# Two attentions that share a memory map: the masks move to the constants, the sums of values to other pools

## The chip, the cores and the metric

The kernel runs on one core of one Trainium2 chip. The metric is the device time of one execution in microseconds. The core has a matrix engine (PE, with its weight loads listed apart as PEld), a vector engine (DVE), a scalar engine (ACT), GpSimd (POOL), and a queue SP from which all transfers of this kernel are issued. Each engine and the queue run their instructions in the order of the program; one that waits holds up all that stand behind it on the same engine. Operands stand in the on-chip memory, which has 128 partitions; addresses below are bytes in a partition.

## The reference

One layer of a hybrid encoder on a sequence of 1024 tokens of width 1024, in float32:

```python
h = rmsnorm(x, attn_norm_g)
(c_q, c_kv, k_rope, z_mla, q_dil, k_dil, v_dil, z_dil, g_mla, g_dil) = jnp.split(h @ w_in, split_points, axis=-1)
a_out = mla_attention(c_q, c_kv, k_rope, positions, mla_q_norm_g, mla_kv_norm_g, w_uq, w_ukv)
y_mla = (a_out * jax.nn.silu(z_mla)) @ w_o_mla
d_out = dilated_mixture(q_dil, k_dil, v_dil, positions)
y_dil = (d_out * jax.nn.silu(z_dil)) @ w_o_dil
merged = gate_mla * y_mla + gate_dil * y_dil
return x + merged @ w_out
```

A final rmsnorm follows. The latent attention has 8 heads, dense and bidirectional; the dilated mixture has 3 groups of 8 heads, of dilation 1, 4 and 16. In the dilated groups every query sees keys within a window only; the kernel adds a mask to the scores for the groups of dilation 1 and 4. The three groups' outputs are combined with softmax weights made of their denominators.

## The kernel before

Every float32 product is made of three matmuls of rounded parts (`mm3`, lines 71 to 73): each operand is split into a high part `_h` (a cast on ACT, line 77) and a low part `_l` (a subtraction, line 78, on DVE or POOL). Every transfer goes through `dma` (line 67), on SP.

The stages, in order of time:

1. `latent_proj`, `tables` and `token_factors` (from 0 us): x is loaded and scaled into `hT_h`, `hT_l`, the latent projections are made, the rotary tables and the row factors R. Then `latents` and `dil_v`, which store q, k and v in DRAM.
2. `blocks`: the projections of q and k of the dilated heads, 12 items (3 groups, two halves of the heads, q and k). The last item is k of the group of dilation 16. `block_steps` copies its result on ACT (line 509) to two tiles `dq_st00` and `dq_st10` and stores them by eight transfers to `s_dk`, the first four from `dq_st00`, the last four from `dq_st10`. Between the engines this stage has an order written out by hand.
3. `dil_attention`: four pairs of heads, for each pair the groups 0, 1, 2. For groups 0 and 1, `dil_head` loads q, k, v (`op_b`, `op_a`, `op_c`), makes scores on PE (lines 808 and 809) into PSUM tiles `s_ps`, and `soft_block` (line 777) adds the mask on DVE, writes `p`, and writes the row minimum into a column of a small tile `d_st`; ACT makes the exponential (line 778). The two halves of an `s_ps` share a bank, so the scores of the second half are written only when line 777 has read the first. `p` is transposed on PE (line 816), split (for group 0 into two large tiles `pt0_h`, `pt0_l`, whose borders POOL sets to zero once, line 1114) and multiplied with v; `av_sum` (line 771) puts the sum into `num`. `combine` weighs and adds the three `num` of a pair (DVE line 964, POOL line 966) and stores the first to `s_da`.
4. `mla_attention`: eight heads in four pairs; `av_sum` writes into a `num` of the pair, `mla_finish` multiplies it with the denominators and stores it to `s_ma` (for the last pair it goes into `brm_h`, `brm_l`, lines 760, 77 and 78).
5. `output`: the last projections and the normalisation. Its gates (`gate`), the rows of w_out (`wo_raw`) and its operands take the memory of the closed pools.

A generator, `fillers`, gives PE other work meanwhile: projections of z and of the gates (tiles `w_raw`, `w_h`, `w_l` for the weights, `pj` in PSUM, `zg_z` and `zg_t` for the result; lines 598 to 605), then the output projection of the dilated branch. 19 steps of it (FIRST_FEED) stand ahead of the dilated attention, the others are handed out behind score and transpose matmuls. From the end of the dilated attention each filler also runs a `piece` (line 582): it loads a part of `s_da` and of z into a `zg_z` and a `zg_t`, multiplies them, and splits the product into `brd_h` (ACT) and `brd_l` (POOL).

The program is written with tiles from pools; outside `blocks` a planner decides the order of each engine's instructions from a simulated run of the program, with the program's order as priority. A tile's place in memory follows from the pools: pools of the left side stand above each other in the order in which they are opened, those of the right side below each other from the top, and inside a pool the tiles stand in the order of their first use, each with its number of buffers. Pools are closed and others opened in their place (`reuse_waits="tile"`): the first write to a tile then waits until the old tiles that lay on the same bytes are done with, and on no others. The places that matter, as the program has them:

| pool (side) | tile: bytes |
|---|---|
| const (left) | warm, consts, rcol: to 1856 |
| op (left, stages 3 and 4) | 1856 to 43840 |
| ap (left, stages 3 and 4) | num 43840 to 60224 (4 x 4096); p, av_t, pt_h, pt_l, bc, m_nm, m_den, m_d to 93312 |
| dx (left, stage 3) | masks 93312; pt0_h 98432; pt0_l 108160; d_st 117888 (2 x 384); c_sn 118656; c_w 121728; c_d 123776 to 125312 |
| brd (left, stage 4) | brd_h 93312; brd_l 109696 to 126080 |
| dt (right, stage 2) | w_raw 75744; st_c 83936; st_t 88032; rope_m0 90080; rope_m1 92128; dq_st00 94176; dq_st10 98272; dq_st01 102368; dq_st11 106464 to 110560 |
| cosd (right, stages 1 and 2) | cs_d 110560 to 118752 |
| zt (right, fillers) | zg_z 126944, 128992; zg_t 131040, 133088 |
| brm (right, from the second part of the fillers) | brm_h 131040, brm_l 147424 to 163808 |
| output (left) | wout_h 10048, wout_l 42816, mg_l 75584, gate 108352 (5 x 2048), wo_raw 118592 (3 x 2048) to 124736 |

Stage 3 has its `num` in four buffers, of which a pair uses three; lines 1108 and 1109 make the tile of the masks, 128 x 1280 float32, as the first of dx and issue its transfer.

Of the kernel before, what the change touches and what calls it, by code (L numbers as in the profile page):

```python
# [10 lines left out]
F32 = mybir.dt.float32  # L11
F32R = mybir.dt.float32r
# [4 lines left out]
PSUM = bass.MemoryType.PSUM  # L17
DRAM = bass.MemoryType.DRAM

S = 1024  # L20
# [31 lines left out]
class Net:  # L52
# [616 lines left out]
    def mla_attention(self, ap, pp):  # L669
        nc = self.nc  # L670
        v = nc.vector
        for pair in range(4):
            num = ap.tile([128, S], F32, name="num", bufs=4)
            nm = ap.tile([128, 2, 8], F32, name="m_nm", bufs=2)
            den = ap.tile([128, 2, 8], F32, name="m_den", bufs=2)
            for hh in range(2):
# [10 lines left out]
                for u in range(4):  # L687
# [3 lines left out]
                    for b2 in range(2):  # L691
# [9 lines left out]
                        p = ap.tile([128, S], F32, name="p", bufs=3)  # L701
# [196 lines left out]
    def dil_attention(self, ap, dx, pp):  # L898
        nc = self.nc
        v = nc.vector  # L900
        for pair in range(4):
            st = dx.tile([128, 3, 2, 2, 8], F32, name="d_st", bufs=2)
            nums = []
            for g in range(3):
                num = ap.tile([128, S], F32, name="num", bufs=4)
                if g == 2:
                    self.dil_classes(pair, st, num, ap, pp)
                    nums.append(num)
                    continue
                for hh in range(2):  # L910
                    self.dil_head(g, pair * 2 + hh, hh, st, num, ap, pp)
                nums.append(num)
            self.combine(pair, st, nums, ap, dx, pp)
# [125 lines left out]
    def run(self):  # L1039
        tc, nc = self.tc, self.nc  # L1040
        with ExitStack() as ctx:
# [12 lines left out]
            cp = ctx.enter_context(tc.tile_pool(name="const", reuse_waits="tile", bufs=1))  # L1054
# [11 lines left out]
            with tc.tile_pool(name="wpx", reuse_waits="tile", bufs=2, side="right") as self.wpx, tc.tile_pool(name="cosd", reuse_waits="tile", bufs=1, side="right") as dpool, ExitStack() as sums:  # L1066
                with tc.tile_pool(name="pj_a", reuse_waits="tile", bufs=NB_A, space=PSUM) as pj, tc.tile_pool(name="dvp", reuse_waits="tile", bufs=3, side="right") as vp:
                    with tc.tile_pool(name="lp", reuse_waits="tile", bufs=1) as lp, tc.tile_pool(name="pj_l", reuse_waits="tile", bufs=8 - NB_A, space=PSUM) as pl:
                        with tc.tile_pool(name="wl", reuse_waits="tile", bufs=1) as wl, tc.tile_pool(name="xp", reuse_waits="tile", bufs=3) as xp:
                            self.latent_proj(lp, wl, xp, pj)  # L1070
                            self.tables(xp)
                            self.token_factors(xp, pl)
                        with tc.tile_pool(name="cosm", reuse_waits="tile", bufs=1) as mpool, tc.tile_pool(name="up", reuse_waits="tile", bufs=1) as lp:
                            self.cos_m, self.sin_m = self.table(mpool, "cs_m", 32)
                            self.cos_d, self.sin_d = self.table(dpool, "cs_d", 0)
                            up = self.up_weights(lp)
                            with tc.tile_pool(name="lt", reuse_waits="tile", bufs=2) as tp:
                                self.latents(up, lp, tp, pl)
                            self.dil_v(0, 0, vp, pj)
                            self.dil_v(0, 1, vp, pj)  # L1080
                    sp = sums.enter_context(tc.tile_pool(name="sums", reuse_waits="tile", bufs=1))
                    with tc.tile_pool(name="bs", reuse_waits="tile", bufs=1) as tp:
                        self.block_sums(sp, tp)
                        self.dil_v(1, 0, vp, pj)
                    for g, quad in ((1, 1), (2, 0), (2, 1)):
                        self.dil_v(g, quad, vp, pj)
                    for x in (self.cos_d, self.sin_d):
                        for half in range(2):
                            c = slice(512 * half, 512 * half + 512)
                            nc.gpsimd.tensor_tensor(out=x[:, c], in0=x[:, c], in1=self.R[:, c], op=ALU.mult)  # L1090
                    z = vp.tile([128, 8, 64], F32, name="zero", bufs=1)
                    nc.gpsimd.memset(z, 0.0)
                    for r in (0, S + 64):
                        self.dma(self.dv[0][r:r + 64].rearrange("r (a b) -> (r a) b", b=512), z.rearrange("p a b -> p (a b)"))
                        for p in range(2):
                            self.dma(self.dk[0][:, :, :, p, r:r + 64].rearrange("h c x t -> (c x) h t"), z[:64])
                with tc.tile_pool(name="dt", reuse_waits="tile", bufs=1, side="right") as tp, tc.tile_pool(name="st", reuse_waits="tile", bufs=1, space=PSUM) as pp:
                    self.blocks([(T_QK + (g * 2 + quad) * 4 + which * 2, g, quad, which) for quad in range(2) for g in range(3) for which in range(2)], tp, pp)
# [6 lines left out]
                next(self.fill)  # L1105
            with tc.tile_pool(name="op", reuse_waits="tile", bufs=1) as self.op, tc.tile_pool(name="ap", reuse_waits="tile", bufs=1) as ap:
                with tc.tile_pool(name="dx", reuse_waits="tile", bufs=1) as dx, tc.tile_pool(name="at_s", reuse_waits="tile", bufs=1, space=PSUM) as self.sp:
                    m = dx.tile([128, 1280], F32, name="masks")
                    self.dma(m, self.a["masks"])
                    self.mask0 = m[:, 0:768].rearrange("p (a b) -> p a b", b=256)  # L1110
                    self.mask1 = m[:, 768:1280].rearrange("p (a b) -> p a b", b=256)
                    self.pt0 = [dx.tile([128, 19 * 128], F32R, name=f"pt0_{c}") for c in "hl"]
                    for x in self.pt0:
                        nc.gpsimd.memset(x.bitcast(F32).rearrange("p (s q) -> p s q", q=128)[:, 0:19:9], 0.0)
                    self.dil_attention(ap, dx, pp)
                with tc.tile_pool(name="brd", reuse_waits="tile", bufs=1) as bp, tc.tile_pool(name="at_s2", reuse_waits="tile", bufs=2, space=PSUM) as self.sp2:
                    self.brd = [bp.tile([128, 4, S], F32R, name=f"brd_{c}") for c in "hl"]
                    self.dil_done = True
                    self.mla_attention(ap, pp)
                    self.stop = True  # L1120
                    for _ in self.fill:
                        pass
# [74 lines left out]
```

## Time and profile before

| | us |
|---|---|
| three runs | 1324.18, 1324.79, 1319.81; median 1324.18 |
| the profiled execution, its own time | 1320.48 |
| its span, first to last instruction | 1318.6 |
| mean granted clock of PE | 0.977 |

The page of the profile gives the busy time of each engine over the span: PE 1249.8 us (95%), DVE 750.9 (57%), ACT 610.4 (46%), POOL 499.5 (38%). Matmuls are pipelined and their ends are modelled, so a busy PE is not PE at its peak. The share is an average over all stages; where PE is idle is seen in the second part of the page, which cuts the span into 40 slices of 33 us and gives one digit for each, in tenths. In the views of the timeline a line begins with the start and the duration in us; what stands in brackets at its end is the idle time of the engine before it and what ended it. In the view of the waits the three numbers are the sum in us, the number of times, and the longest.

### The profile page before, as it was taken

Reading aid. Unit: us, or ns where it says so; the run is one execution under the profiler, and the core shown is the slowest. Engines: PE = TensorE matmul, PEld = TensorE weight load, DVE = VectorE, ACT = ScalarE, POOL = GpSimd, SP = SyncE. Lnnn points to the kernel's source line nnn. Section 1 sums busy time; section 2 is a strip of 40 time slices with the busy share of each in tenths; the row PEclk is TensorE's granted clock in tenths of the full one; section 3 lists DMA queues with packets and bytes.
Section 4 is the critical chain, followed back from the end, with each engine's and each line's share of the span. In section 5 each row is a group of like instructions: output and inputs, shape, how many; then the busy total and the mean of one; then the engine's idle time right before and its main releaser. Section 6 shows DMA issues by size and latency. Waiting matters only on the chain.

```text
span 1318.6 us, 19629 instructions
## 1 busy us (share of the span) xinstructions
PE 1249.8 (95%) x6957; PEld 1082.7 (82%) x6957; DVE 750.9 (57%) x1359; ACT 610.4 (46%) x1276; POOL 499.5 (38%) x393
## 2 busy tenths in 40 slices
PE   8999999999999959988899899999999999999998
PEld 7898998888888848877778788888888888887786
DVE  7463526476476624657465575856565556559522
ACT  6533356343444325545355463455555555454322
POOL 3251229777777523436222041212111022136522
PEclk9999999999999979999989899999999999999999
DMA  9757583467457676677875878545333364136322
GB/s 315 242 169 293 210 276 108 132 157 168 120 138 165 160 195 160 174 181 202 209 204 137 216 208 204 146 141 160 97 97 104 97 176 132 62 121 221 126 95 71
DMA packets 132898, 217.26 MB, mean 165 GB/s; under 512 B 36984, under 2 KB 66240, under 8 KB 128896
## 3 DMA queue, kind: packets, MB, share of 16 engines
q1 hardware_dynamic: 132800, 216.01, 57.8%
q8 instruction: 55, 0.90, 0.3%
q14 instruction: 43, 0.35, 0.1%
HBM read 147.21 MB, written 68.75 MB: 164 GB/s over the span
## 4 chain that ended last, share of the span: by engine, by line
PE 65%; DMA 14%; DVE 5%; issue 3%; POOL 2%; SPq 2%; ACT 1%; DVEq 0%; ACTq 0%; POOLq 0%
PE pj L71 9%; PE pj L72 9%; PE pj L73 9%; PE pt L713 4%; DMA s_sd<-av_t 3%; DMA op_a<-s_dk 3%; PE av L722 2%; PE av L721 2%; PE s_mla L71 2%; SPq L67 2%; PE s_mla L73 2%; PE s_mla L72 2%; PE st_a L71 2%; PE st_a L73 2%; PE st_a L72 2%
## 5 line engine op out<-in xcount | busy, mean ns | idle before, releaser
L78 POOL TENSOR_TENSOR w_l<-w_raw,w_h 128x512 fp32r<-128x512 f32 (+1 forms) x176 | 232.6, 1330 | 452.5 <-ACT w_h L77 383.4
L78 DVE TENSOR_TENSOR pt_l<-pt,pt_h 128x512 fp32r<-128x512 f32 x192 | 131.7, 687 | 89.6 <-ACT pt_h L77 87.7
L77 ACT CAST pt_h<-pt 128x512 fp32r<-128x512 f32 x192 | 112.1, 584 | 128.5 <-PE pt L713 57.6
L71 PE MATMUL pj<-hT_h,w_h 128*128 128x512 f32 x384 | 167.0, 435 | 1.8 <-DVE zg_z L598 1.8
L72 PE MATMUL pj<-hT_l,w_h 128*128 128x512 f32 x384 | 153.7, 400 | 0.0
L73 PE MATMUL pj<-hT_h,w_l 128*128 128x512 f32 x384 | 153.7, 400 | 0.0
L77 ACT CAST w_h<-w_raw 128x512 fp32r<-128x512 f32 (+1 forms) x176 | 106.1, 614 | 100.8 <-POOL w_raw L415 65.0
L72 PE MATMUL pj<-w_l,hT_h 128*128 128x256 f32 x384 | 108.9, 284 | 0.0
L73 PE MATMUL pj<-w_h,hT_l 128*128 128x256 f32 x384 | 108.9, 284 | 0.0
L71 PE MATMUL pj<-w_h,hT_h 128*128 128x256 f32 x384 | 108.6, 283 | 0.0
L699 DVE TENSOR_REDUCE m_nm<-s_mla 128x1 f32<-128x1024 f32 x64 | 78.0, 1220 | 30.6 <-PE s_mla L73 30.3
L778 ACT ACTIVATE p<-p,d_st 128x256 f32<-128x256 f32 x128 | 64.4, 504 | 66.4 <-DVE d_st L777 66.2
L73 PEld LDWEIGHTS pj<-hT_h,w_l 128*128 128x128 f32 x384 | 74.1, 193 | 16.6
L777 DVE CUSTOM_DVE_ANT_0 p<-s_ps,masks 128x256 f32<-128x256 f32 x128 | 51.0, 417 | 63.8 <-PE s_ps L809 27.4
L71 PEld LDWEIGHTS pj<-hT_h,w_h 128*128 128x128 f32 x384 | 75.0, 195 | 12.5 <-DVE zg_z L598 2.5
L72 PEld LDWEIGHTS pj<-hT_l,w_h 128*128 128x128 f32 x384 | 75.1, 196 | 10.0
L702 ACT ACTIVATE p<-s_mla,m_nm 128x1024 f32<-128x1024 f32 x64 | 71.8, 1122 | 23.2 <-PE pt L713 16.3
L713 PE MATMUL pt<-consts,p 128*128 128x128 f32 x512 | 78.7, 274 | 1.1 <-ACT p L702 1.1
L71 PEld LDWEIGHTS pj<-w_h,hT_h 128*128 128x128 f32 x384 | 73.5, 191 | 0.9
L72 PEld LDWEIGHTS pj<-w_l,hT_h 128*128 128x128 f32 x384 | 73.5, 191 | 0.8
L73 PEld LDWEIGHTS pj<-w_h,hT_l 128*128 128x128 f32 x384 | 73.4, 191 | 0.9
L721 PE MATMUL av<-pt_h,op_c 128*128 128x256 f32 x256 | 69.0, 289 | 1.4 <-ACT pt_h L77 1.4
(303 smaller groups left out, 3240.3 us busy)
## 6 DMA issues: line engine op xcount, KB each, us to landing
w_raw<-wt SPq DMA_DIRECT2D x48, 512.0 KB, 3.6
op_b<-s_dq SPq DMA_DIRECT2D x32, 512.0 KB, 8.8
s_dq<-dq_st SPq DMA_DIRECT2D x80, 128.0 KB, 2.4
s_dk<-dq_st SPq DMA_DIRECT2D x80, 128.0 KB, 2.4
gate<-s_gt SPq DMA_DIRECT2D x34, 256.0 KB, 2.9
s_dv<-dv_st SPq DMA_DIRECT2D x32, 256.0 KB, 3.8
s_gt<-zg_t SPq DMA_DIRECT2D x32, 256.0 KB, 3.0
w_raw<-wv SPq DMA_DIRECT2D x12, 512.0 KB, 6.1
```

Source lines behind the costliest of these rows:

```text
L67: self.nc.sync.dma_start(out=out, in_=in_)
L71: mm(out, lh, rh, start=start, stop=False, skip_group_check=skip)
L72: mm(out, lh, rl, start=False, stop=False, skip_group_check=skip)
L73: return mm(out, ll, rh, start=False, stop=stop, skip_group_check=skip)
L77: self.nc.scalar.copy(out=h, in_=raw)
L78: sub.tensor_tensor(out=l, in0=raw, in1=h.bitcast(F32), op=ALU.subtract)
L699: v.tensor_reduce(out=nm[:, hh, qb:qb + 1], in_=s, axis=AX.X, op=ALU.max, negate=True)
L702: nc.scalar.activation(out=p, in_=s, func=AF.Exp, bias=nm[:, hh, qb:qb + 1], accum_out=den[:, hh, qb:qb + 1])
L713: self.anchor = nc.tensor.transpose(pt[:, o:o + 128], P[b2][:, 128 * kc:128 * kc + 128], self.ident)
L721: nc.tensor.matmul(a_out, vv[:, kc], ph[:, s], start=kc == 0, stop=False)
L777: nc.vector.tensor_tensor_reduce(out=p, in0=s, in1=mask, op0=ALU.add, op1=ALU.min, scale=-0.125, scalar=3e38, accum_out=nm)
L778: nc.scalar.activation(out=p, in_=p, func=AF.Exp, scale=-1.0, bias=nm, accum_out=den)
```

## The change

Three edits:

- the tile of the masks is made in the pool of the constants, at the end of the first stage, behind `token_factors`, and its transfer is issued there in the program's order; it is kept to the end;
- the dilated attention's `num` (four buffers) moves from ap to dx;
- the latent attention's `num` moves from ap to the pool of `brd`, with two buffers, behind `brd_h` and `brd_l`.

No computation is added or left out.

```diff
@@ mla_attention
         for pair in range(4):
-            num = ap.tile([128, S], F32, name="num", bufs=4)
+            num = self.bp.tile([128, S], F32, name="num", bufs=2)
@@ dil_attention
             for g in range(3):
-                num = ap.tile([128, S], F32, name="num", bufs=4)
+                num = dx.tile([128, S], F32, name="num", bufs=4)
@@ run
                             self.tables(xp)
                             self.token_factors(xp, pl)
+                            m = cp.tile([128, 1280], F32, name="masks")
+                            self.dma(m, self.a["masks"])
+                            self.mask0 = m[:, 0:768].rearrange("p (a b) -> p a b", b=256)
+                            self.mask1 = m[:, 768:1280].rearrange("p (a b) -> p a b", b=256)
@@ run
                 with tc.tile_pool(name="dx", reuse_waits="tile", bufs=1) as dx, tc.tile_pool(name="at_s", reuse_waits="tile", bufs=1, space=PSUM) as self.sp:
-                    m = dx.tile([128, 1280], F32, name="masks")
-                    self.dma(m, self.a["masks"])
-                    self.mask0 = m[:, 0:768].rearrange("p (a b) -> p a b", b=256)
-                    self.mask1 = m[:, 768:1280].rearrange("p (a b) -> p a b", b=256)
                     self.pt0 = [dx.tile([128, 19 * 128], F32R, name=f"pt0_{c}") for c in "hl"]
@@ run
-                with tc.tile_pool(name="brd", reuse_waits="tile", bufs=1) as bp, tc.tile_pool(name="at_s2", reuse_waits="tile", bufs=2, space=PSUM) as self.sp2:
-                    self.brd = [bp.tile([128, 4, S], F32R, name=f"brd_{c}") for c in "hl"]
+                with tc.tile_pool(name="brd", reuse_waits="tile", bufs=1) as self.bp, tc.tile_pool(name="at_s2", reuse_waits="tile", bufs=2, space=PSUM) as self.sp2:
+                    self.brd = [self.bp.tile([128, 4, S], F32R, name=f"brd_{c}") for c in "hl"]
```

## The prediction

> **What bounds the kernel now.** I read the page first. PE is busy nearly everywhere; its digits (one for each 33 us) show one slice at half:
>
> ```profile
> PE   8999999999999959988899899999999999999998
> ```
>
> The 5 is slice 14, from 461 to 494 us, where the dilated attention begins. Second, the waits of the stretch from 455 to 512 us, longest first; third, the chain of work that ended last, in the same stretch (start, duration):
>
> ```profile
> POOL pt_h L1114 <- DMA s_dk<-dq_st: 23.2, 1, 23.2
> DVE p L777 <- DMA masks<-masks: 19.6, 1, 19.6
> ```
>
> ```profile
> 480.71 2.44 DMA s_dk<-dq_st
> 483.24 3.81 DMA masks<-masks
> 487.19 0.42 DVE p L777
> ```
>
> The reader is to see two things. DVE waits 19.6 us for the masks, but their transfer is only 3.81 us of it: it starts when the last store of `dq_st` has landed (480.71 + 2.44 = 483.15), since the tile of the masks lies on `dq_st00` and `dq_st10`. And POOL waits 23.2 us for the same store, at the zeroing of `pt0_h` (the views leave digits out of names: pt_h), which reads nothing of it; it too only needs the memory. Last, PE and POOL in the timeline:
>
> ```profile
> 474.02 0.39 PE L73 MATMUL pj<-hT_h,w_l 128*128 128x512 f32 x1
> 487.68 0.58 PE L808 MATMUL s_ps<-op_a,op_b 128*128 128x256 f32 x1 [13.27 <-DVE d_st L777]
> ...
> 490.83 0.63 PE L73 MATMUL pj<-hT_h,w_l 128*128 128x512 f32 x1
> 491.26 0.63 PE L71 MATMUL pj<-hT_h,w_h 128*128 128x512 f32 x1
> ```
>
> ```profile
> 483.29 0.42 POOL L1114 MEMSET pt_h<- 128x384 f32 x1 [23.16 <-DMA s_dk<-dq_st]
> 483.64 0.42 POOL L1114 MEMSET pt_l<- 128x384 f32 x1
> 484.02 1.26 POOL L601 TENSOR_TENSOR zg_t<-zg_t,zg_z 128x512 f32<-128x512 f32 x1
> 485.36 1.26 POOL L602 TENSOR_TENSOR zg_t<-zg_t,zg_z 128x512 f32<-128x512 f32 x1
> 486.58 1.27 POOL L78 TENSOR_TENSOR w_l<-w_raw,w_h 128x512 fp32r<-128x512 f32 x1
> ```
>
> PE stands still for 13.27 us, until line 777 has read the first half of a score tile. So the prize seems to be 13 to 19 us. It is not, as the places of the tiles show.
>
> **The change part by part.** *The wait for the masks.* The masks leave dx, so none of the 3.81 us is left there. What is late next? I lay the tiles out anew, from the table of places. The constants grow by 5120 bytes, so op starts at 6976 and ap at 48960; ap is 16384 smaller and ends at 93312 + 5120 - 16384 = 82048, where dx begins: `pt0_h` 82048 to 91776, `pt0_l` to 101504, `d_st` 101504 to 102272, then four `num` to 118656. The pools of the right side don't move, and `dq_st10` has 98272 to 102368. So `d_st`, which lay on `cs_d` before, now lies on `dq_st10` with both buffers, and line 777 writes `d_st`. The eight stores are issued in order, `dq_st10` last, so line 777 waits for the very store that the masks waited for: until 483.15, and as POOL's memset starts 0.14 after it, DVE starts at 483.29 instead of 487.19. **Gain at this gate: 3.90 us**, not 13.
>
> *What takes some of it back.* POOL's second memset writes `pt0_l`, now on `dq_st00` and `dq_st10`, so POOL is held until 483.15 as before; only the first memset (0.35 from start to start) goes ahead, since `pt0_h` now lies on tiles that DVE has done with after 466.29 + 0.69:
>
> ```profile
> 466.29 0.69 DVE L491 TENSOR_TENSOR st_a<-st_a,rope_m 128x512 f32<-128x512 f32 x1
> ```
>
> Behind it the low part of the next weights ends at 486.58 + 1.27 - 0.35 = 487.50. The first matmul that needs it is that of 490.83, which with the full gain would start at 486.93. It waits 0.57 us: **the gain is 3.33 us**, bounds 0 (POOL's order gets worse by as much) and 7.8 (the first rival below). The second half of these weights is needed only by matmuls behind the next scores, so I cost it at nothing; POOL's time for it is the cover. From there PE carries the chain, and I take the rest of the dilated stage as moved as a whole.
>
> *The clock.* The granted clock, third number from the end, in single microseconds:
>
> ```profile
> 479.00:480.00 1.00, 0.00 (x0) 0.00 (x0) 0.00 (x0) 0.00 (x0) 0.00 (x0) 0.76 1.02 410
> 480.00:481.00 1.00, 0.00 (x0) 0.00 (x0) 0.00 (x0) 0.00 (x0) 0.00 (x0) 0.50 0.85 324
> ...
> 493.00:494.00 1.00, 1.00 (x6) 0.83 (x5) 0.00 (x0) 0.00 (x0) 0.71 (x1) 0.92 0.69 270
> ```
>
> It falls to half at about 479.5, 5.1 us after PE stopped at 474.4, and comes back at about 493.1, 5.4 us after the restart. With the change PE is idle from 474.4 to 483.8 (0.49 behind DVE, as before), 9.4 us, beyond those 5.1, so the restart is at half clock as before: no term. [...]
>
> *The masks in the first stage.* One transfer of 128 x 1280 x 4 = 655360 bytes is added to the load there. Nothing there holds it up, so the planner may issue it wherever its simulated queue is free, while x and weights are still being loaded:
>
> ```profile
> 25.00:30.00 5.00, 5.00 (x29) 5.00 (x28) 5.00 (x6) 3.73 (x7) 2.81 (x2) 1.00 1.05 387
> ```
>
> ```profile
> 28.87 1.14 ACT L77 CAST w_h<-w_raw 128x512 fp32r<-128x512 f32 x2 [1.01 <-DMA w_raw<-wv]
> 30.04 1.28 ACT L222 ACT_TABLE_LOAD   x1
> 33.41 1.06 ACT L222 ACTIVATE cs<-ang 64x1024 f32<-64x1024 f32 x1 [2.09 <-DVE ang L220]
> ```
>
> The transfers are saturated (share 1.05) at 387 GB/s, so what stands behind comes 1.69 us later. If that is the weights for ACT at 28.87, ACT has 2.09 us of idle time at 33.41 to take it in; if it is a piece of x, PE may lose it. Bounds 0 and 1.7 (nothing is saved, as bytes are added); I take **0.3 back**, near the covered end.
>
> *The latent attention's tiles.* By the same arithmetic `brd_h` lies at 82048, `brd_l` at 98432 to 114816, the two `num` at 114816 and 118912. The low parts of the pieces now wait for all four old `num`, the first of which is read by the last store to `s_da`:
>
> ```profile
> s_da<-num SPq DMA_DIRECT2D x4, 512.0 KB, 8.6
> ```
>
> ```profile
> 848.43 0.32 SPq L67 DMA_DIRECT2D s_da<-num  x1
> ...
> 850.80 0.38 SPq L67 DMA_DIRECT2D zg_z<-s_da  x1
> ```
>
> ```profile
> 847.11 1.29 POOL L966 TENSOR_TENSOR num<-num 128x512 f32<-128x512 f32 x1 [1.10 <-DVE num L964]
> 848.37 1.75 POOL L78 TENSOR_TENSOR w_l<-w_raw,w_h 128x512 fp32r<-128x512 f32 x1
> 850.08 1.29 POOL L78 TENSOR_TENSOR brd_l<-zg_z,brd_h 128x512 fp32r<-128x512 f32 x1
> 859.16 1.28 POOL L78 TENSOR_TENSOR brd_l<-zg_z,brd_h 128x512 fp32r<-128x512 f32 x1 [7.79 <-ACT brd_h L77]
> ```
>
> ```profile
> 851.21 0.67 DVE L771 TENSOR_TENSOR num<-av,av_t 64x512 f32<-64x512 f32 x1
> ```
>
> The store lands at 848.43 + 8.6 = 857.0, so the first `brd_l` moves from 850.08 to 857.0. Behind it on POOL stands only the second, which isn't due before 859.16 and which POOL awaits idle for 7.79: cost **0**, bounds 0 and 7 (see the slower rival). The first `num` lies on the `num` of group 1 and on `c_sn`; POOL's last sum ends at 847.11 + 1.29 = 848.40, and line 771 writes at 851.21: no wait.
>
> *The end.* `gate` and `wo_raw` move up by 5120. Three of the five gates then lie on the last `num`, which is read until 1183.92 + 1.02 = 1184.94:
>
> ```profile
> 1183.92 1.02 DVE L78 TENSOR_TENSOR brm_l<-num,brm_h 128x512 fp32r<-128x512 f32 x1 [0.69 <-ACT brm_h L77]
> ```
>
> ```profile
> 1183.73 0.43 SPq L67 DMA_DIRECT2D gate<-s_gt  x1
> 1184.20 0.43 SPq L67 DMA_DIRECT2D wo_raw<-w_out  x1
> ```
>
> The third gate would be issued 1.2 us later, and with it the `wo_raw` behind it. Bounds 0 and 1.2; I take **0.2**, since the planner can send the other first.
>
> **Sum**: -3.33 + 0.3 + 0 + 0.2 = -2.8 us. On the profiled execution's own 1320.48 us that is 1317.7. It was a fast one: the runs are 1324.18, 1324.79 and 1319.81. On their median the forecast is **1321.4 us**.
>
> **The rivals.** *POOL lets go as well (faster).* `pt0_h` is free early; if the planner now puts lines 601, 602 and the subtraction ahead of the second memset, the weights are ready before 478, and PE does, while it would be idle, the filler matmuls that ran at half clock from 489.83 on. Of the 19 steps ahead of the attention 16 use up two halves of a weight tile and three are left, nine matmuls; at 491.26 - 490.83 = 0.43 us each they are 3.9, with the 3.90 of the gate 7.8: 1324.2 - 7.8 + 0.5 = 1317, on the edge of faster. Against it: the same three stood behind both memsets before, though ready sooner.
>
> *The pieces stall DVE (slower).* If the second piece's `zg_z` gets the buffer that the first piece holds, its load can't be issued at 850.80 but only when `brd_l` has been written, at 858.3, and as the row below shows, DVE stands in order behind that load:
>
> ```profile
> 857.74 0.69 DVE L582 TENSOR_TENSOR zg_z<-zg_z,zg_t 128x512 f32<-128x512 f32 x1 [4.13 <-DMA zg_z<-s_da]
> ```
>
> The load took 857.7 - 850.8 = 6.9 us, so line 582 would start at 865.2, 7.5 late, with the transposes' splits behind it. Less the 2.8: 1324.2 + 4.7 = 1329. It decides against the change once the delay exceeds 2.8 us. Against it: at 850.80 the load was issued before the first `brd_l` had ended (851.4), so it had another buffer.
>
> *The masks' transfer hits x.* The whole 1.7 in the first stage: 1322.8. *The change does nothing.* Another wait, of POOL or of a store that lands later, takes the 3.3 as well: 1324.7.
>
> *Another plan.* New places and one transfer elsewhere change the planner's simulated run, and so orders far from the change. The size comes from stalls that this order has, one more or less of
>
> ```profile
> 37.02 0.46 PE L71 MATMUL pj<-wl_h,hT_h 128*128 128x416 f32 x1 [3.12 <-ACT hT_h L150]
> 101.15 0.79 PE L71 MATMUL pj<-lat_h,uq_h 128*128 128x512 f32 x1 [3.02 <-DVE mla_st L313]
> ```
>
> and the 13.27: 3 to 13 us either way.
>
> **How the numbers follow.** About 0.5% (6.6 us) is what a measurement of this kernel can tell from no change: below 1317.6 is faster, above 1330.8 slower. Forecast 0.40; POOL lets go 0.13; the pieces 0.14; the first stage 0.08; nothing 0.10; another plan 0.15, half of it on each side. Faster: 0.08 of POOL's, 0.06 of the plans, and 0.06 of the forecast, as the runs before lie at 1320 and 1324: 0.20. Slower: a third of the pieces' and the slower plans: 0.12. Same: 0.68. The range leaves out the outer parts of the plans on both sides: 1312 to 1332.
>
> **What would show it.** In the changed profile DVE's first line 777 waits for `s_dk<-dq_st`, not for a load, and starts within 0.3 us of POOL's second memset; PE's idle time there is 9 to 10 us; the masks land before 40 us and PE's wait at 37 us is no longer than 5; the first `brd_l` follows the landing of the last `s_da`. Wrong is the forecast if line 777 starts before that store lands (then `d_st` lies elsewhere than I worked out), or if a wait of over 3 us appears on PE, or on DVE ahead of PE, between 850 and 870.

## The result and the profile after

| | before | after |
|---|---|---|
| runs | 20 | 20 |
| median (us) | 1321.72 | 1313.34 |
| lowest to highest | 1317.12 to 1328.71 | 1309.58 to 1320.48 |
| profiled execution, own time | 1320.48 | 1310.85 |
| its span, mean granted clock | 1318.6, 0.977 | 1309.0, 0.979 |

The ratio of the times is 0.9939, with a 95% interval of 0.9923 to 0.9956: the change gains about 8 us, between 6 and 10. The direction and the range were right. The size was not (2.8 us were forecast), nor was the likeliest class, "within 0.5%". The time of 1321.4 us stood 8.1 above the measured median: 5.6 of it are missing gain, and 2.5 are the base, for the three runs that the forecast started from have their median at 1324.18 and the twenty at 1321.72.

The waits of the kernel after between 455 and 512 us, the three that answer to those shown of before (sum, times, longest):

```profile
DVE p L777 <- DMA s_dk<-dq_st: 15.3, 1, 15.3
POOL pt_l L1114 <- DMA s_dk<-dq_st: 11.4, 1, 11.4
PE s_ps L808 <- DVE d_st L777: 9.0, 1, 9.0
```

DVE at line 777 waits for the last store of `dq_st` in place of the masks. The chain that ended last shows the landing, 475.75 + 2.52 = 478.27, and what starts behind it:

```profile
475.75 2.52 DMA s_dk<-dq_st
...
478.50 0.42 DVE p L777
...
478.99 0.58 PE s_ps L808
```

PE's timeline has the stop at its two ends, and POOL's shows that the two zeroings have come apart: the one of `pt0_h` runs early, that of `pt0_l` waits for the same store.

```profile
469.61 0.39 PE L73 MATMUL pj<-hT_h,w_l 128*128 128x512 f32 x1
478.99 0.58 PE L808 MATMUL s_ps<-op_a,op_b 128*128 128x256 f32 x1 [8.98 <-DVE d_st L777]
```

```profile
465.27 1.28 POOL L601 TENSOR_TENSOR zg_t<-zg_t,zg_z 128x512 f32<-128x512 f32 x1 [9.55 <-ACT zg_t L600]
466.49 0.42 POOL L1114 MEMSET pt_h<- 128x384 f32 x1
478.32 0.42 POOL L1114 MEMSET pt_l<- 128x384 f32 x1 [11.41 <-DMA s_dk<-dq_st]
478.70 1.28 POOL L602 TENSOR_TENSOR zg_t<-zg_t,zg_z 128x512 f32<-128x512 f32 x1
```

That is the gate, worth 13.27 - 8.98 = 4.29 us of PE's idle time. But the two executions are apart before it. Rows of PE's timeline, before first, then after (in brackets the wait that ended there):

```profile
226.24 0.50 PE L71 MATMUL st_a<-hT_h,w_h 128*128 128x512 f32 x1 [3.29 <-ACT dv_s L376]
...
467.71 0.39 PE L808 MATMUL s_ps<-op_a,op_b 128*128 128x256 f32 x1 [1.18 <-ACT dq_st L509]
...
509.07 0.35 PE L808 MATMUL s_ps<-op_a,op_b 128*128 128x256 f32 x1 [2.00 <-DMA op_a<-s_dk]
```

```profile
102.00 0.50 PE L71 MATMUL pj<-lat_h,uq_h 128*128 128x512 f32 x1 [1.76 <-DVE mla_st L313]
...
223.08 0.50 PE L71 MATMUL st_a<-hT_h,w_h 128*128 128x512 f32 x1 [0.92 <-ACT dv_s L376]
...
463.30 0.39 PE L808 MATMUL s_ps<-op_a,op_b 128*128 128x256 f32 x1 [1.18 <-ACT dq_st L509]
...
499.32 0.36 PE L808 MATMUL s_ps<-op_a,op_b 128*128 128x256 f32 x1 [1.55 <-DMA op_a<-s_dk]
```

The first score matmul of the dilated attention comes at 463.30 instead of 467.71, 4.41 us sooner, ahead of the gate. About 2.7 us of it are less idle time of PE. The rest is the granted clock (third number from the end in the rows below, before first, then after): the profile before has two stretches of half clock on the way, 3.41 us each, around 102 and 228 us; that after has one, at 36 us.

```profile
101.00:104.00 3.00, 2.85 (x7) 2.27 (x8) 1.18 (x3) 0.96 (x2) 0.00 (x0) 0.50 0.63 231
227.00:230.00 3.00, 3.00 (x8) 2.31 (x8) 2.79 (x2) 2.07 (x5) 3.00 (x3) 0.50 0.14 46
```

```profile
101.00:104.00 3.00, 2.00 (x11) 1.74 (x12) 1.80 (x4) 1.55 (x4) 0.00 (x0) 1.00 0.66 245
227.00:230.00 3.00, 3.00 (x15) 2.45 (x14) 1.75 (x2) 1.19 (x3) 3.00 (x2) 1.00 0.13 44
```

From the first score matmul to the row that waits for a load of `op_a` (499.32, before 509.07) the same work takes 36.0 us instead of 41.4, 5.3 less. Together these are 9.75 us, and the profiled executions differ by 1320.48 - 1310.85 = 9.63. So in this pair all is won by 500 us, nearly half of it in a stage for which the prediction had a loss of 0.3. Why is what the experiments had to settle. Two figures sort them: the time of **the first score matmul**, and **the gate's stretch**, from it to the row that waits for `op_a`.

### The profile page after: what moved, and what is told of

The parts are those of the page before. It is cut to its first block, busy times and chain, and to the rows that moved or that the text cites. A ratio compares the mean times of both kernels' runs of the same rounds, so it can differ in the third digit from the quotient of the medians.

```text
span 1309.0 us, 19640 instructions
## 1 busy us (share of the span) xinstructions
PE 1246.4 (95%) x6957; PEld 1080.9 (83%) x6957; DVE 756.0 (58%) x1359; ACT 609.6 (47%) x1276; POOL 499.5 (38%) x393
## 4 chain that ended last, share of the span: by engine, by line
PE 66%; DMA 12%; DVE 6%; issue 4%; POOL 3%; ACT 1%; SPq 1%; DVEq 0%; POOLq 0%; ACTq 0%
PE pj L71 10%; PE pj L72 10%; PE pj L73 10%; PE pt L713 4%; DMA s_sd<-av_t 3%; DMA op_a<-s_dk 3%; PE av L722 2%; PE av L721 2%; PE s_mla L71 2%; PE s_mla L72 2%; PE s_mla L73 2%; PE st_c L73 2%; PE st_c L71 2%; PE st_c L72 2%; PE st_d L72 2%
```

## The experiments

Four theories were tested. **A**: two gains, one from the masks' transfer in the first stage, which lets the planner's order of the stages ahead of the gate come out better, one from the gate. **B**: the upstream gain comes from the shift of all places by 5120 bytes. **C**: the upstream gain is the spread between two executions. **D**, formed after the eighth run: DVE and POOL hold each other up between 66 and 84 us, by chance.

All results in one table. The ratio is to the kernel before on the same chip, with its 95% interval.

| run | masks loaded | places at the gate | first score matmul | gate's stretch | ratio |
|---|---|---|---|---|---|
| before | late | masks, d_st as before | 467.71 | 41.4 | 1 |
| after | early | d_st over dq_st10 | 463.30 | 36.0 | 0.9939 (0.9923 to 0.9956) |
| 1 num only | late | as after | 467.80 | 38.9 | 0.9981 (0.9956 to 1.0005) |
| 2 load twice | early and late | as before | 461.95 | 39.2 | 0.9979 (0.9948 to 1.0009) |
| 3 const, late in the text | early | as after | 466.90 | 36.7 | 0.9958 (0.9937 to 0.998) |
| 4 low d_st, bc and m_nm moved | early | nothing over dq_st | 464.52 | 27.6 | 1.0062 (1.004 to 1.0084) |
| 5 low d_st, bc moved | early | nothing over dq_st | 468.64 | 26.0 | 0.9905 (0.9883 to 0.9927) |
| 6 low d_st, masks late | late | nothing over dq_st | 467.78 | 38.3 | 0.9997 (0.9974 to 1.002) |
| 7 tiny load | tiny early, late | as before | 467.94 | 40.9 | 1.0016 (0.9996 to 1.0037) |
| 8 after again | early | as after | 468.77 | 36.2 | 0.9949 (0.9923 to 0.9975) |
| 9 low d_st, line 277 on ACT | early | nothing over dq_st | 460.68 | 26.3 | 0.9868 (0.9847 to 0.989) |
| 10 low d_st, cs_d on DVE | early | nothing over dq_st | 468.93 | 26.7 | 0.993 (0.9904 to 0.9956) |
| 11 run 5 again | early | nothing over dq_st | 466.95 | 26.2 | 0.9898 (0.9865 to 0.993) |
| 12 after, line 277 on ACT | early | as after | 459.69 | 36.4 | 0.9916 (0.988 to 0.9953) |

What matters ahead of the gate is the order in which the planner puts each engine's instructions. Up to the first score matmul the traces have PE, DVE, ACT and POOL in the order of the kernel after in runs 2, 4, 5, 8 and 11, and in that of the kernel before in runs 1 and 6. Runs 3, 7 and 10 have orders of their own, and runs 9 and 12 one in common.

### 1. The moves of num alone

```diff
 # the kernel after, with the old place of the masks
-                            m = cp.tile([128, 1280], F32, name="masks")
+                    m = dx.tile([128, 1280], F32, name="masks")
```

> The kernel after, but the masks loaded at the old place, by the dilated attention into a tile of dx (now at 76928, over w_raw, free early); num stays in dx and brd, so d_st lies at 101504 over dq_st10 as in the kernel after. Theory A (two gains: the masks' transfer in the first stage lets the order written ahead of the run come out otherwise, -4.4 us by the first score matmul; and the gate waits for a store in place of the masks, -4.3): first matmul of s_ps at 467.7 as before, PE idle ahead of the second score matmul about 9 us in place of 13.3, in all -4 to -5 us, 0.9965 of before. Theory B (the shift of all places by 5120 bytes brings the -4.4): the same here, -4 to -5, for const isn't longer. Theory C (the -4.4 is only the spread between two runs and the gate is worth all of it): -8, 0.994.

Measured: the first score matmul at 467.80, the wait 11.89 us, the ratio 0.9981. The upstream part is as A and B said; the gate is not as any theory said. The masks' tile, at 76928, lay on memory that is free early, and yet DVE waited 18.24 us for the masks. SP's own rows of this run show why (start, duration):

```profile
471.87 9.03 SPq L67 DMA_DIRECT2D s_dk<-dq_st  x8
480.94 0.42 SPq L67 DMA_DIRECT2D masks<-masks  x1
```

The load stands behind the eight stores **in SP's queue**, and they are issued only when `dq_st` has been written. So the masks had two reasons to be late, memory and queue, and moving the tile takes away only one.

### 2. The masks loaded twice

```diff
 # the kernel before
                             self.token_factors(xp, pl)
+                            m = xp.tile([128, 1280], F32, name="masks_x", bufs=1)
+                            self.dma(m, self.a["masks"])
```

> The kernel before with one transfer more: the masks are also loaded in the first stage, behind token_factors, into a tile of pool xp that nothing reads; const, dx, ap and the latent attention's tiles are those of before. Theory A: the first matmul of s_ps comes at about 463.3 as in the kernel after, DVE still waits for the masks' second transfer at line 777 and PE idles about 13 us there; in all -4.4 us, 0.9967 of before. Theory B: no place below dx has changed, so s_ps at 467.7, and 1.000 of before, or up to 0.3 us slower by the transfer. Theory C: 1.000.

Measured: 461.95, 12.40 us of idle time at the gate, 0.9979. The places of const, op, ap and dx are those of before, yet the first score matmul moved by 5.8 us, and up to it every engine has the order of the kernel after. So the new order comes with the early transfer and not with the places: B falls. The transfer of 640 KB itself cost nothing that shows. The interval of the time (0.9948 to 1.0009) holds A's 0.9967 as well as no gain.

### 3. The masks in const, loaded late in the text

```diff
 # the kernel after
-                            self.dma(m, self.a["masks"])
...
+                    self.dma(m, self.a["masks"])
                     self.pt0 = [dx.tile([128, 19 * 128], F32R, name=f"pt0_{c}") for c in "hl"]
```

(The tile of const is made there too.)

> The kernel after, but the tile of the masks in const is loaded where before loaded them, at the opening of dx: all places of op, ap, dx and brd are those of the kernel after, only the transfer has moved. Theory A: no early transfer, so no gain upstream: s_ps at 467.7; the masks' load waits for nothing any more and the gate is the store's, about 9 us: -4 to -5 us in all, 0.9965 of before. Theory B: s_ps at 463.3 and the gate at 9 us: -8 to -9 us, 0.9935. Theory C: -8 without a gain upstream.

Measured: 466.90, 8.78 us, 0.9958. The premise did not hold. The view of the masks' tile in this run has its one transfer (duration in ns, start):

```profile
L67 SPq DMA_DIRECT2D masks<-masks x1: 622/622/622, 29.7 to 29.7; - x1
```

A tile of const has no earlier owner, so the planner issued the load at 29.7 us wherever it stood in the text. The run says nothing between A and B; it says that what brings the masks early is that nothing stands in their memory, not the line's place.

### 4. pt0 and d_st off dq_st, bc and m_nm moved

`bc`, `m_nm`, `m_den` and `m_d` leave ap, which brings dx down by 8512 bytes.

```diff
 # the kernel after
-                r = ap.tile([128, 512], F32, name="bc", bufs=NB_BC)
+                r = dx.tile([128, 512], F32, name="bc", bufs=NB_BC)
...
-            nm = ap.tile([128, 2, 8], F32, name="m_nm", bufs=2)
+            nm = self.bp.tile([128, 2, 8], F32, name="m_nm", bufs=2)
```

> The kernel after with bc, m_nm, m_den and m_d taken from dx and brd in place of ap: pt0_h, pt0_l and d_st come down to 73536 to 93760, where w_raw, st_c, st_t and rope_m lay, and none of them lies over a dq_st whose store is late. Theory A (DVE's wait at line 777 is for the store of s_dk alone): that wait goes, PE's idle time ahead of the second score matmul falls from 9 us to under 3, and 5 to 7 us more are gained: 0.988 to 0.990 of before. Rival (POOL's w_l and its memset of pt0_l, or the second load of op_b, are as late): the wait only changes its name, and the time stays that of the kernel after, 0.994 of before.

Measured: the gate's wait is gone and its stretch is 27.6 us, as A said; but the kernel is slower than before, 1.0062. The loss is one row of PE, at the start of the latent attention:

```profile
828.11 0.69 PE L713 MATMUL pt<-consts,p 128*128 128x128 f32 x2 [26.02 <-ACT p L702]
```

and DVE's rows say what it waits for:

```profile
821.34 4.21 DVE L964 TENSOR_TENSOR num<-num,bc 128x512 f32<-128x512 f32 x3 [0.23 <-DMA bc<-s_rr]
825.47 2.34 DVE L699 TENSOR_REDUCE m_nm<-s_mla 128x1 f32<-128x1024 f32 x2
```

The first row maximum writes `m_nm`, which now lay at 114496, on `c_w` of the last `combine`, and came on DVE only behind that pair's last multiplication. 128 bytes cost PE 26 us of idle time.

### 5. and 11. The same with m_nm left in ap

```diff
 # the kernel after: bc alone moves
-                r = ap.tile([128, 512], F32, name="bc", bufs=NB_BC)
+                r = dx.tile([128, 512], F32, name="bc", bufs=NB_BC)      # combine
+                r = self.bp.tile([128, 512], F32, name="bc", bufs=NB_BC) # latent attention
```

Every engine's order is that of the kernel after; the places alone differ. The eleventh run is the same program again.

> The kernel after with only bc moved from ap to dx (dilated attention) and to the pool of brd (latent attention); m_nm, m_den and m_d stay in ap, so that the latent attention's first row maxima no longer wait for the memory of the dilated bc. pt0_h, pt0_l and d_st come down to 73856 to 94080, below dq_st00; each engine's order is that of the kernel after. Theory A (the gate's wait for the store is 9 us of PE's idle time, held by the places alone; the 26 us that the run before lost at 828 came from m_nm over bc): PE waits under 3 us ahead of the second score matmul, the third pair of scores starts near 492 in place of 499, no wait of over 4 us at 800 to 860, and the time is 6 to 9 us below the kernel after: 0.988 to 0.990 of before. Rival (another stage gives it back): the scores of the dilated stage come 7 us earlier and the end does not: 0.994, as the kernel after.

> The fifth run once more, on the chip of the two beside it. All theories: 0.990 of before (0.988 to 0.993), PE's wait at the gate under 3 us. Theory D: line 277 takes another length than the 13.6 us that it took in the first profile of this kernel, anywhere from 9 to 14, and the first matmul of s_ps moves with it, between 463 and 469.

Measured: 0.9905 and 0.9898, at the upper end of what A said (0.988 to 0.990), 5 to 6 us below the kernel after. (The expectation names `bc` as what `m_nm` lay on; by the places it was `c_w`. The 26 us are gone.) DVE now reads the first scores at once, and the next wait of PE is a load:

```profile
469.18 0.42 DVE L777 CUSTOM_DVE_ANT_0 p<-s_ps,masks 128x256 f32<-128x256 f32 x1 [0.69 <-PE s_ps L809]
```

```profile
494.65 0.55 PE L808 MATMUL s_ps<-op_a,op_b 128*128 128x256 f32 x1 [2.79 <-DMA op_a<-s_dk]
```

The stretch is 26.0 and 26.2 us: the places of `d_st` and `pt0_l` had been holding 10 us. Some of it is given back at the end. From the last line 633 on DVE to the first line 999 there pass 16.8 us before and 16.9 after, and 19.5 and 18.6 in these two runs: three of the gates lie on the latent attention's `bc` now, and their loads are issued later.

### 6. The low places with the masks late

> The first experiment (num moved, masks loaded at the old place in dx) with bc moved as in the run before, so that pt0, d_st and the masks lie below dq_st00, with no early transfer; each engine's order is that of the first experiment. Theory A (the two gains add up and are independent): upstream as before, first s_ps at 467.7; PE's idle time ahead of the second score matmul falls from 11.9 us to under 3; 8 to 11 us gained against before, 0.992 to 0.994. Rival (the upstream gain is what lets the gate come early): 0.997, as the first experiment.

```diff
 # the kernel of run 1
-                r = ap.tile([128, 512], F32, name="bc", bufs=NB_BC)
+                r = dx.tile([128, 512], F32, name="bc", bufs=NB_BC)      # combine
+                r = self.bp.tile([128, 512], F32, name="bc", bufs=NB_BC) # latent attention
```

Every engine's order is that of run 1. Measured: 11.10 us of idle time and 0.9997, so A's "independent" is wrong. With all the memory free DVE still waits 17.46 us for the masks, which stand behind the stores on SP as in run 1, and the end gives 2.5 us back (19.3 against 16.8). With the masks late the stretch is 38.9 us with the places of after and 38.3 with the low ones; with the masks early it is 36.0 and 26.0. The low places are worth 0.6 us in the one case and 10 in the other. **Gains behind one gate don't add up; the last condition sets the time.** (Run 2 says nothing on this: its early copy is read by nobody, and DVE waits for the late one.)

### 7. A tiny load

```diff
 # the kernel before
+                            m = xp.tile([128, 1280], F32, name="masks_x", bufs=1)
+                            self.dma(m[:, 0:16], self.a["masks"][:, 0:16])
```

> The kernel before with a transfer of 128 x 16 of the masks (8 KB instead of 640 KB) added at the end of the first stage, into a tile that nothing reads. Theory A1 (the early transfer's own size, by the time that it takes up in the planner's simulated queue, brings about the better order): the order of before, s_ps at 467 to 468, 1.000. Theory A2 (any added transfer makes the planner choose otherwise, and the choice is a matter of chance): an order of its own, with s_ps anywhere between 461 and 473 and a time within 0.5% of before on either side.

Measured: an order of its own, and nothing gained: 467.94, 1.0016. So 8 KB are enough to make the planner choose otherwise, as A2 said, and the choice may come to nothing. Whether the 640 KB of run 2 lead to a better order by their size or by luck these two runs don't tell.

### 8. The kernel after once more

> The kernel after, unchanged, on the same chip as the three runs beside it, so that they can be compared with it. All theories: 0.994 of before, first s_ps at 463 to 464, 9 us idle ahead of the second score matmul. Theory C (the gain upstream was chance of one run): s_ps at 466 to 468.

Measured: 0.9949, the gate 8.45 us, as expected; but the first score matmul at 468.77, 5.5 us later than in the first profile of the *same program*, and 1.1 later than before. That is C's side, and beyond it. Windows of both profiles (window, length, busy time of PE, PEld, DVE, ACT and POOL with counts, granted clock, DMA share, GB/s), the first profile, then this run:

```profile
76.00:80.00 4.00, 2.27 (x19) 2.07 (x19) 4.00 (x7) 0.50 (x2) 4.00 (x4) 1.00 0.15 55
80.00:84.00 4.00, 4.00 (x36) 4.00 (x35) 3.89 (x7) 0.76 (x2) 3.61 (x3) 1.00 0.80 239
```

```profile
76.00:80.00 4.00, 1.96 (x9) 1.52 (x9) 4.00 (x5) 0.00 (x0) 3.90 (x4) 0.59 0.00 0
80.00:84.00 4.00, 3.85 (x20) 3.70 (x20) 4.00 (x14) 1.74 (x3) 0.00 (x0) 0.55 0.12 44
```

In run 8 PE starves here and the clock falls to half. DVE is all but full in every window: from 71.8 to 82.3 us in run 8, and from 68.9 to 78.2 in the first profile, it works through line 277, which scales `lat` in 16 instructions. The rows of that line (ns of one: least, median, most; first and last start) in the kernel after, in run 5 and in run 9, where ACT does it:

```profile
L277 DVE TENSOR_SCALAR lat<-lat,rs_y x16: 278/346/1393, 68.9 to 76.8; 128x256 f32<-128x256 f32 x8, 128x128 f32<-128x128 f32 x8
```

```profile
L277 DVE TENSOR_SCALAR lat<-lat,rs_y x16: 274/1288/1866, 69.2 to 82.6; 128x256 f32<-128x256 f32 x8, 128x128 f32<-128x128 f32 x8
```

```profile
L277 ACT ACTIVATE lat<-lat,rs_y x16: 384/446/511, 66.8 to 74.5; 128x256 f32<-128x256 f32 x8, 128x128 f32<-128x128 f32 x8
```

and POOL beside it in run 5:

```profile
70.08 5.15 POOL L1094 TENSOR_TENSOR cs_d<-cs_d,R 128x512 f32<-128x512 f32 x4 [17.93 <-DMA u_raw<-wuq]
75.19 1.29 POOL L78 TENSOR_TENSOR w_l<-w_raw,w_h 128x512 fp32r<-128x512 f32 x1
76.44 1.89 POOL L78 TENSOR_TENSOR uq_l<-u_raw,uq_h 128x768 fp32r<-128x768 f32 x1
```

On DVE an instruction of 0.27 to 0.35 us takes up to 1.87 in run 5, and these are POOL's lengths: 1.29 and 1.89 us. Line 277 takes 4.9, 6.0 and 7.1 us in the profiles with the order of before (runs 1, before, 6), and 9.3, 10.5, 13.6, 9.3, 9.3 and 10.9 with that of after (after, 8, 5, 11, 2, 4). It starts 2.4 to 3.4 us ahead of POOL's work in the first group, and 0.8 to 1.4 ahead (3.8 behind in run 8) in the second; of the orders of their own, run 7 has 8.2 us by 1.8 ahead and run 3 13.6 by 1.0. In the kernel after five of the 16 take 1.37 to 1.39 us: each starts while an instruction of POOL runs and ends 0.1 us behind it, the first at 70.52 + 1.39 = 71.91, beside POOL's 70.30 + 1.52 = 71.82. There POOL's four multiplications of `cs_d` are longer too, 1.60 us in the median against 1.31 in run 1; in run 5 they have 1.32.

This is theory D, and the traces let its cost be summed: PE's idle time between 60 and 95 us, and half of the time there in which it works at half clock. That comes to 0.1 to 0.5 us in the order of before, and in that of after to 1.7 (run 2), 1.8 (after), 4.8 (11), 5.0 (4), 7.7 (5) and 8.4 (8). In these six profiles of one order the first score matmul lies between 461.95 and 468.77; less this cost it lies between 459.5 and 462.1. Most of the spread is the contest's.

Elsewhere the order of after is the better one. The waits around 101 and 226 us, 6.3 to 7.1 us together in the order of before, come to 1.2 to 4.1, and of the two stretches of half clock beside them, which all three profiles of before's order have, five of the six have none (run 11 has both). Less the contest, the first score matmul lies at 460.8 in the mean of the six and at 467.5 in that of the three: the order itself is worth 6.7 us, and the contest that comes with it takes 1.7 to 8.4 of them back. As measured, the six have a mean of 465.7, and before's order has it at 467.71, 467.80 and 467.78. So the upstream gain is **2.1 us in the mean**, with 7 us of spread (six profiles fix that mean to no better than about 1 us), and not the 4.4 of the first pair.

### 9. and 12. Line 277 on ACT

```diff
-                    v.tensor_scalar(out=c[:, s], in0=c[:, s], scalar1=f, scalar2=None, op0=ALU.mult)
+                    nc.scalar.mul(c[:, s], c[:, s], f)
```

in run 5 (run 9) and in the kernel after (run 12). The two have the same order on every engine.

> The fifth run (masks early, pt0, d_st low) with line 277's scaling of lat, 16 instructions, done by ACT in place of DVE. Theory D (between 66 and 84 us DVE's line 277 and POOL's multiplications of cs_d and subtractions hold each other up, an instruction of DVE waiting for a whole one of POOL; so line 277 takes 5 to 14 us by chance, PE runs out of other matmuls and the clock drops): the PE wait at 73 to 85 us (up to 6 us in four of the profiles) is gone or under 2, no half clock there, s_ps begins at 461 to 465 in this profile, and the median falls 2 to 4 us below the fifth run, 0.987 to 0.989 of before. Rival (the wait is DVE's own length, or comes from the landing of R): ACT is as late, the wait stays and so does the time, 0.990.

> The kernel after with line 277's scaling of lat on ACT, all places as in the kernel after; each engine's order is that of the ninth run, which differs in the places alone. Theory D (the contest of DVE and POOL costs the new order some 3 to 5 us by chance, the gate's store 4 to 5 us more, and the two add up): s_ps at 460 to 462, 8.5 to 9.5 us idle ahead of the second score matmul, and a median between the kernel after and the ninth run, 0.990 to 0.992 of before. Rival (what is won upstream is lost again at the gate, as the stores land when they do): the gate opens as late as in the kernel after, 0.994.

Measured: 0.9868 and 0.9916, the first score matmul at 460.68 and 459.69, no idle time of PE and no half clock between 60 and 95 us, and none of the 16 over 0.51 us (run 9) with POOL as busy as before (13.70 us of work between 66 and 84 us in run 12, 13.35 in the kernel before). D holds as far as the gate. (The edit also gives a new order; but the first score matmul lies where the six profiles have it less the contest, 459.5 to 462.1.)

Behind the gate less is shown. Run 12 has the gate's 8.57 us as the kernel after has it, and its profile is 3.2 us ahead of that of the kernel after at the row that waits for `op_a` (496.13 against 499.32); but the last score matmul of the dilated attention starts at 793.61 (after: 794.21), and the two executions took 1310.84 and 1310.85 us. What took the 3.2 back in that stage stays open, and the interval of run 12's time (0.988 to 0.9953) holds D's 0.991 as well as the rival's 0.994. **Run 9, with a median of 1304.77 us, beats both kernels**: 1.3% below before, and by the ratios (0.9868 to 0.9939) 0.7% below after. Its interval overlaps those of runs 5 and 11, so the share of line 277 in that time is told by the trace and not by the time.

### 10. cs_d on DVE

```diff
-                            nc.gpsimd.tensor_tensor(out=x[:, c], in0=x[:, c], in1=self.R[:, c], op=ALU.mult)
+                            nc.vector.tensor_tensor(out=x[:, c], in0=x[:, c], in1=self.R[:, c], op=ALU.mult)
```

(in run 5)

> The fifth run with the four multiplications of cs_d and sn_d by R, that stand on POOL beside line 277, given to DVE (four of about 0.69 us each in place of 1.3 us on POOL); line 277 stays on DVE. Theory D: fewer POOL instructions beside line 277, so it takes 5 to 9 us, the PE wait there is under 3 us, and the median is 1 to 4 us below the fifth run, 0.987 to 0.990 of before. Rival: DVE is the bound of this stretch by itself; four instructions more make line 277 later by 2.8 us, and the time is that of the fifth run or up to 3 us longer, 0.990 to 0.993.

Measured: 0.993, the rival's upper end. DVE now waits 2.75 us for a landing, does the four multiplications in two pairs, the second slowed beside POOL's remaining subtractions (2.95 us, the first 1.29), and line 277 starts at 76.6 where it had started at 69.2:

```profile
68.36 1.29 DVE L1094 TENSOR_TENSOR cs_d<-cs_d,R 128x512 f32<-128x512 f32 x2 [2.75 <-DMA u_raw<-wuq]
...
69.73 2.95 DVE L1094 TENSOR_TENSOR cs_d<-cs_d,R 128x512 f32<-128x512 f32 x2
...
76.61 3.55 DVE L277 TENSOR_SCALAR lat<-lat,rs_y 128x256 f32<-128x256 f32 x8
```

Of the two sides of the contest DVE is the one that PE waits for; the work taken from POOL stood ahead of line 277 there.

## Why the prediction was right and where it failed

**The gate: right.** `d_st` lay where the table of places had put it, line 777 waited for the store of `dq_st10`, and DVE started 0.18 us behind POOL's second memset (within 0.3 was forecast). PE's idle time fell by 4.29 us (3.90 was forecast, and "9 to 10" left; it was 8.98). That this change's prize is 3 to 5 and not 13 to 19 was the most useful line of the prediction, and run 5 shows it: with `d_st` and `pt0_l` elsewhere the wait is gone.

**What was taken back: wrong, too small a gain.** The step "it waits 0.57 us: the gain is 3.33" failed; the gate's stretch is 5.3 us shorter in the first pair (4.29 at the gate, 0.6 by the clock, and 0.45 at the wait for `op_a`, 1.55 for 2.00) and 5.1 in run 8. POOL put line 601 ahead of the memset that waits, the start of the "POOL lets go" rival, and PE shows no wait at all between the second scores and 499.32. The bounds, 0 and 7.8, held it.

**The clock: half at the restart, as said, but for 3.4 us less.** Single microseconds of the kernel after:

```profile
472.00:473.00 1.00, 0.00 (x0) 0.00 (x0) 0.00 (x0) 0.00 (x0) 0.00 (x0) 1.00 1.06 286
473.00:474.00 1.00, 0.00 (x0) 0.00 (x0) 0.00 (x0) 0.00 (x0) 0.00 (x0) 0.50 1.08 410
...
483.00:484.00 1.00, 1.00 (x5) 0.87 (x4) 0.00 (x0) 0.59 (x4) 1.00 (x2) 0.88 0.00 0
```

Half clock lasts from 473.0 to 483.24, 10.2 us; before it was 479.5 to 493.1, 13.6 us. Behind the restart PE runs at half clock for 4.2 us instead of 5.4: 0.6 us of the gain, which "no term" left out.

**The masks in the first stage: the step that failed.** "I take 0.3 back, near the covered end" treated the edit as one transfer more. The transfer, issued at 20.25 us, cost nothing. What it did was in the rival "another plan": other orders to 460 us, which run 2 shows to come with the transfer alone. In the profiled pair they gave 4.4 us, in the mean of six profiles 2.1. The rival was given 0.15, half on each side, and its size was read from the waits at 37 and 101 us; the one at 101 did shrink, and so did that at 226, which was not quoted, and with them the half clock beside them. That the new order also brings a wait which the old one did not have (line 277 beside POOL, 1.7 to 8.4 us) was foreseen by no part. That the range of 1312 to 1332 held the median, 1.3 us above its lower end, is luck in part: this piece came out on its faster side.

**The latent attention and the end: right.** The first `brd_l` waits 2.07 us for `brd_h` and starts at 844.35; the second `zg_z` does not wait longer than before (3.37 us, before 4.13):

```profile
849.51 0.69 DVE L582 TENSOR_TENSOR zg_z<-zg_z,zg_t 128x512 f32<-128x512 f32 x1 [3.37 <-DMA zg_z<-s_da]
```

So `brd_l` did not start behind the landing of the last `s_da` as "what would show it" had it: it starts 3.75 us behind that store's issue (840.60), and the forecast's 8.6 us were the one recorded landing, of an earlier store. The cost of 0 was right. The slower rival did not come: the load of the second `zg_z` was issued at 842.95, ahead of the first `brd_l` (844.35), so it had its own buffer. At the end 16.9 us pass from line 633 to line 999 where 16.8 had passed: the 0.2 was 0.1.

**The sum.** On average the gate's stretch gives 5.2 and the orders upstream 2.1, 7.3 of the 8.4 us by the medians; the interval of the change (6 to 10) and that of its repetition (0.9923 to 0.9975, 3 to 10 us) hold that. The 1 us between is not accounted for: single profiles spread by more. The forecast had 2.8 because it took the gate 2 us too small and gave the first stage a loss of 0.3 where 2.1 were gained.

## What to carry to other kernels

When a wait has several conditions (memory, a queue, another engine), list them all with their times; an edit that removes one shows the next, and only the edit that removes the last one shows the prize (41.4, 36.0, 26.0 us here). Of a tile that is moved, check the small tiles as well: 768 bytes of `d_st`, with `pt0_l` beside them, on the wrong place cost 10 us at the gate (no run moves one of the two alone), and 128 bytes of `m_nm` 26. With a planner that orders instructions anew, compare several profiles of each order before an upstream difference is believed: the same program had its first score matmul at 463.30 and at 468.77. And compare the orders themselves: runs 2 and 4 had the order of the kernel after though their places differ.

## What the runs showed of the hardware

- An instruction of DVE that takes 0.27 to 0.35 us alone took 1.37 to 1.39 beside POOL in the kernel after, each ending 0.1 us behind an instruction of POOL, and up to 1.94 (run 3), and the sum of 16 such lay between 4.9 and 13.6 us with their relative start; ACT, at 0.45 us each in the median and 0.51 at most (run 9), was not touched.
- The stretches of half clock around the gate last 13.65 and 10.24 us, four and three times 3.413. Between 20 and 1290 us the traces of before and after have 19 such stretches, of 3.41, 6.83, 10.24 or 13.65 us, and in each trace their starts and ends lie whole multiples of 3.413 us apart.
- PE's idle time ahead of the fall was 5.1 us in the kernel before and 473.0 - 470.0 = 3.0 in the kernel after (matmul ends are modelled), so the 5.1, which the prediction had read as a threshold, is none. Cut into steps of 3.413 us at those starts and ends, between 20 and 1290 us, the two traces have 19 steps at full clock that a fall follows, with 1.39 to 3.41 us of PE's idle time in them, and no other step at full clock has more than 1.89.
